# Weight places and loads of 8 KB a partition, and one float32 product in place of three fp32r ones

## Chip, cores and metric

The program runs on one core of one Trainium2 chip. The metric is the device time of one execution in microseconds (us). Engines: TensorE does the matrix products (PE, with PEld for its weight loads), VectorE (DVE), ScalarE (ACT) and GpSimd (POOL) work element by element, SyncE (SP) issues most of the DMA transfers. A "record" is one instruction in the trace.

## What is computed

One decoder layer on 512 tokens of width 1024, all of it float32: a projection whose columns feed four causal mixers (SSD, RWKV7, GLA, mLSTM), an output projection, LayerNorm, a router that sends each token to 4 of 32 experts, the experts, a gate, and LayerNorm again. Cut to what matters here:

```python
u = x @ w_in                                    # 1024 -> columns of the four mixers
u_ssd, u_rwkv, u_gla, u_mlstm = _split(u, (SSD_W, RWKV_W, GLA_W, MLSTM_W))
...
mix = jnp.concatenate([y_ssd, y_rwkv, y_gla, y_mlstm], -1) @ w_out      # 1024 x 1024
x = _layer_norm(DEEPNORM_ALPHA * x + mix, ln1_g, ln1_b)
# experts: top 4 of 32, weights per expert w_gu 1024 x 2048, w_down 1024 x 1024
hg, hl = jnp.split(xblk @ w_gu[e] + b_gu[e], 2, axis=-1)
hg, hl = jnp.minimum(hg, 7.0), jnp.clip(hl, -7.0, 7.0)
y = ((hl + 1.0) * (hg * jax.nn.sigmoid(hg * 1.702))) @ w_down[e] + b_down[e]
...
h = DEEPNORM_ALPHA * x + ffn
h = h + jax.nn.sigmoid(h @ ple_gate_w) * (p @ ple_proj)                 # the last gate
x = _layer_norm(h, ln2_g, ln2_b)
```

## The kernel before

**The front (0 to about 405 us).** `mixers()` computes the projections and the four mixers. A projection is done in blocks. `split()` (L149 to L159) loads 512 KB of weights through SP, ScalarE copies them rounded to the type fp32r (`wh`, L157), and VectorE takes what the rounding left (`wl`, L158). The tokens `x` are split in the same way into `x0h` to `x3h` and `x0l` to `x3l`. `proj()` makes one of 18 blocks (tile `pj`, 128 x 512) out of three products of parts, wh x, wl x and wh xl, each over 8 steps of k (128 rows of the 1024): 24 matmuls of one record each, at the helper's line L144. `projt()` makes 5 groups of 4 blocks with the tokens on the partitions (`pt`, 128 x 256, again 24 matmuls a block). The mixers' outputs are split too (`finish_tm`, and for RWKV7 where `yo` is made, L487 to L492), since the output projection (`mixed()` and `wout()`, tile `mix`) is 3 x 64 such matmuls. In the middle of the front runs RWKV7's recurrence: eight steps, each of them U = W Tt, then S and WO from VU, then W for the next step, with copies on VectorE between them. A scheduler lays out the order of the instructions on each engine in the front; it fills the gaps with blocks of projections.

**The experts (about 405 to 1497 us).** `moe()` takes the 32 experts in the order of a table. An expert's tokens come in groups of 32: 18 experts have three groups and 14 have two. For a group `up()` multiplies by the gate and up weights (tile `gu`, L1297), `swiglu()` follows on VectorE and ScalarE, and `down()` multiplies again (tile `dn`, L1308); each product of 32 tokens uses a quarter of the array, so four run side by side. An expert has 24 units of weights of 128 x 1024 (4 KB a partition, 512 KB). They stand in a ring of 32 places, made of four pools (14 `rb`, 8 `r2`, 2 `wr`, 8 `r3`), four more while the front ends. `used()` marks a place as free and `pump()` at once issues the next load into it through SP (L1229); 15 units are loaded ahead while the front still runs. These float32 products are not split. The layer's second input goes through the same ring (`embed()`, tile `emb`, L1356: float32 products of 128 x 512), and so do the 8 units of the last gate's weights.

**The tail (1497 to 1577 us).** `gateweights()` splits the last gate's weights, `transposed()` (L1552 to L1555) brings 128 rows of `h` onto the partitions and splits them as `hh` (ScalarE) and `hl` (VectorE), and `finish()` makes three matmuls a step (L1596, L1597, L1598), sigmoid, LayerNorm and the stores.

Of the kernel before, what the change touches and what calls it, by code (L numbers as in the profile page):

```python
# [14 lines left out]
ALU = mybir.AluOpType  # L15
# [21 lines left out]
OPT = {"conv": ("sx0",), "lnt": ("vv","va","aa","va"), "lov": ("zb",), "pl": (0,5,8,13,16,21), "pt": (), "em": 20, "wk": 6, "ml": 0, "hold": 0, "gm": (0,), "pe": 0, "order": "SABZDIgvLqmoM", "wm": (10,8,0), "bn": (), "ad": (), "rb": (2,0,3), "pf": {(0,1):15}, "ex": 4, "xq": 1, "aq": 1,  "ap": 2, "t1": (8,8), "pa": 1,  "op": ((2,1),(0,))}  # L37
# [89 lines left out]
def mixers(tc, nc, A, rbp, dram, mix, ctx, ident, ones, tri, x1d, accd, R, dbg):  # L127
# [110 lines left out]

    def projt(name):

        i = GI[name]
        w = [split(A["wT"][i, h], [128, 4, 256], "w") for h in range(2)]
        for c in range(NT):
            tk = slice(128 * c, 128 * c + 128)
            p = ps("p", "pt")
            n = 0
            for a, b in ((0, xh), (1, xh), (0, xl)):
                for k in range(KT):
                    mm(p[:, 0:256], b[k // 2][:, k % 2, tk], w[k // 4][a][:, k % 4], start=(n == 0), stop=(n == 3 * KT - 1))
                    n += 1  # L250
            yield p[:, 0:256]
# [3 lines left out]
    def finish_tm(name, k, i, y, tag, pt="m"):  # L255

        if k // 2 not in Y:
            Y[k // 2] = (tl(tag, W2, name + "h", F32R), tl(tag, W2, name + "l", F32R))
        yh, yl = Y[k // 2]
# [5 lines left out]
        s.activation(yh[:, :, tk], pp_, AF.Copy)  # L265
        R["done"] = v.tensor_sub(yl[:, :, tk], pp_, yh[:, :, tk].bitcast(F32)).ins
# [14 lines left out]
    def rwkv():  # L281
# [106 lines left out]
        AQ = tl("rb", [128, 32, 32], "AQ")  # L388
# [39 lines left out]
        for c in range(8):  # L428
# [54 lines left out]
            yo = tl("rd", [128, 2, 128], "yo")  # L483
# [3 lines left out]
            v.tensor_mul(yo, yo, gg[:, :, t2])  # L487
            if i == 0:
                Y[1] = [tl("rb", W2, "y_rwkv" + x, F32R) for x in "hl"]
            Yr = Y[1]  # L490
            s.activation(Yr[0][:, :, t2], yo, AF.Copy)
            v.tensor_sub(Yr[1][:, :, t2], yo, Yr[0][:, :, t2].bitcast(F32))  # L492
# [566 lines left out]
def moe(ctx, tc, nc, A, ident, rbp, R, x1d, accd, ovt, ove, out, dbg):  # L1059
# [62 lines left out]
    wg = []  # L1122

    def gateweights():

        for k in range(KT):
            w = ring[len(srcs) - KT + k]
            pool, tag, n = [(R["pools"]["r3"], "r3", RING3), (R["pools"]["wr"], "wr", SLOTS["wr"])][k] if k < 2 else (rbp, "rb", SLOTS["rb"])
            hi, lo = (pool.tile([128, D], F32R, name=x, tag=tag, bufs=n) for x in ("wh", "wl"))
            s.activation(hi, w, AF.Copy)  # L1130
            v.tensor_sub(lo, w, hi.bitcast(F32))
            wg.append((hi, lo))


# [569 lines left out]
```

## Times and profile before

| | us |
|---|---|
| three runs | 1573.88, 1576.99, 1579.82 (median 1576.99) |
| the profiled execution | 1578.24 |
| its span, first to last instruction | 1576.4 |
| PE busy in it | 1462.9 (93%) |
| DVE, ACT, POOL busy | 522.9, 301.7, 218.2 |
| mean granted TensorE clock | 0.961 of full |
| DMA, mean over the span | 296 GB/s, 148012 packets |

The profiled execution lies 1.25 us above the median. PE is the busiest engine over the whole, yet that is a mean over stages: the DMA engines are nearly idle in the front and in the tail, and full for the 1056 us of the experts. The stages must be read apart. PE's busy time counts a matmul to its modelled end, so records overlap: the pitch of records that follow one another (start to start) is what one costs.

### The profile page before, as it was taken

Reading aid. Unit: us, or ns where it says so; the run is one execution under the profiler, and the core shown is the slowest. Engines: PE = TensorE matmul, PEld = TensorE weight load, DVE = VectorE, ACT = ScalarE, POOL = GpSimd, SP = SyncE. Lnnn points to the kernel's source line nnn. Section 1 sums busy time; section 2 is a strip of 40 time slices with the busy share of each in tenths; the row PEclk is TensorE's granted clock in tenths of the full one; section 3 lists DMA queues with packets and bytes.
Section 4 is the critical chain, followed back from the end, with each engine's and each line's share of the span. In section 5 each row is a group of like instructions: output and inputs, shape, how many; then the busy total and the mean of one; then the engine's idle time right before and its main releaser. Section 6 shows DMA issues by size and latency. Waiting matters only on the chain. (4 is left out here: it accounts for less than half of the span.)

```text
span 1576.4 us, 36036 instructions
## 1 busy us (share of the span) xinstructions
PE 1462.9 (93%) x14672; PEld 776.0 (49%) x14672; DVE 522.9 (33%) x1597; ACT 301.7 (19%) x632; POOL 218.2 (14%) x222
## 2 busy tenths in 40 slices
PE   9989999997799999999999999999999998999985
PEld 5769879886244433443334333334434343334364
DVE  5688875668521112111121111111121111111155
ACT  4343523523011111110111110101111110111120
POOL 1011211003011211211111111111111211111100
PEclk9899999997899999999999999999999999999998
DMA  4222311654979999999999999999999999999931
GB/s 165 61 67 64 113 44 52 235 224 159 346 275 366 360 387 393 380 390 379 381 384 382 369 380 376 383 382 378 335 389 388 379 387 373 390 380 392 390 104 42
DMA packets 148012, 466.13 MB, mean 296 GB/s; under 512 B 27121, under 2 KB 36162, under 8 KB 147810
## 3 DMA queue, kind: packets, MB, share of 16 engines
q1 hardware_dynamic: 131666, 442.08, 74.2%
q0 software_dynamic: 14992, 18.90, 5.8%
q8 instruction: 117, 1.92, 0.5%
q10 hardware_dynamic: 1184, 2.80, 0.5%
q14 instruction: 53, 0.43, 0.1%
HBM read 452.08 MB, written 18.43 MB: 298 GB/s over the span
## 5 line engine op out<-in xcount | busy, mean ns | idle before, releaser
L1297 PE MATMUL gu<-w,x 128*32 128x512 f32 x5248 | 627.4, 596 | 22.7 <-DMA w<-in_we_dram 21.7
L1297 PEld LDWEIGHTS gu<-w,x 128*32 128x32 f32 x5248 | 189.1, 119 | 442.6 <-issue 292.8
L1316 DVE TENSOR_SCALAR a<-gu 128x256 f32<-128x256 f32 x82 | 34.8, 425 | 895.8 <-PE gu L1297 895.8
L1308 PE MATMUL dn<-w,h 128*32 128x256 f32 x5248 | 304.0, 387 | 0.6 <-issue 0.6
L1308 PEld LDWEIGHTS dn<-w,h 128*32 128x32 f32 x5248 | 160.4, 112 | 121.0 <-issue 8.7
L1327 POOL DMA_INDIRECT accd<-y,ixs x82 | 128.0, 1561 | 357.9 <-ACT y L1326 330.2
L1317 ACT ACTIVATE c<-a 128x256 f32<-128x256 f32 x82 | 34.2, 417 | 631.7 <-DVE a L1316 630.1
L1208 POOL DMA_INDIRECT xg<-x1d,ixt x32 | 32.8, 1025 | 585.2 <-PE tr L1279 524.1
L1326 ACT ACTIVATE y<-dn,gate 128x256 f32<-128x256 f32 x82 | 36.7, 473 | 273.2 <-PE dn L1308 273.2
L1279 PE MATMUL tr<-ident,xg 96*128 96x96 f32 (+1 forms) x256 | 31.6, 251 | 31.3 <-ACT h L1267 18.1
L1279 PEld LDWEIGHTS tr<-ident,xg 96*128 96x128 f32 (+1 forms) x256 | 22.6, 142 | 42.3 <-ACT h L1267 24.8
L158 DVE TENSOR_TENSOR wl<-w,wh 128x1024 fp32r<-128x1024 f32 x28 | 34.2, 1220 | 15.0 <-ACT wh L157 14.9
L1320 DVE TENSOR_TENSOR b<-b,c 128x256 f32<-128x256 f32 x82 | 34.9, 425 | 5.4
L1264 PE MATMUL tr<-ident,b 128*128 128x128 f32 x164 | 32.3, 298 | 4.7 <-DVE b L1320 1.6
L1319 DVE SCALAR_TENSOR_TENSOR b<-b,a 128x256 f32<-128x256 f32 x82 | 34.5, 421 | 1.8
L157 ACT ACTIVATE wh<-w 128x1024 fp32r<-128x1024 f32 x28 | 29.5, 1053 | 25.6 <-PE pj L144 17.4
L1280 ACT ACTIVATE x<-tr 128x384 f32<-128x384 f32 (+1 forms) x64 | 27.7, 443 | 34.2 <-PE tr L1279 33.2
L1318 DVE TENSOR_SCALAR b<-gu 128x256 f32<-128x256 f32 x82 | 34.0, 415 | 0.0
L1267 ACT ACTIVATE h<-tr 128x256 f32<-128x256 f32 x82 | 29.4, 381 | 15.1 <-PE tr L1264 12.2
L1089 DVE TENSOR_SCALAR pt<-iotas,rankm 128x384 bf16<-128x384 bf16 (+1 forms) x132 | 30.9, 295 | 0.0
L1289 PEld LDWEIGHTS <-sel 96*32 96x32 bf16 x656 | 17.8, 98 | 21.7 <-issue 9.9
L1596 PE MATMUL gu<-wh,hh 128*128 128x512 f32 (+1 forms) x72 | 27.6, 387 | 0.3 <-ACT hh L1554 0.3
(650 smaller groups left out, 1683.5 us busy)
## 6 DMA issues: line engine op xcount, KB each, us to landing
w<-in_we_dram SPq DMA_DIRECT2D x768, 512.0 KB
w<-in_wA_dram SPq DMA_DIRECT2D x18, 512.0 KB
w<-in_wT_dram SPq DMA_DIRECT2D x10, 512.0 KB
wo<-in_wO_dram SPq DMA_DIRECT2D x8, 512.0 KB
w<-in_pgw_dram SPq DMA_DIRECT2D x8, 512.0 KB
x<-in_xT_dram SPq DMA_DIRECT2D x4, 512.0 KB
xt<-in_xt_dram SPq DMA_DIRECT2D x4, 512.0 KB
x1d<-xt ACTq DMA_DIRECT2D x4, 512.0 KB
```

The lines of the kernel that those rows point to most:

```text
L158: v.tensor_sub(wl, w, wh.bitcast(F32))
L1208: return g.indirect_dma_start(out=xg[TURN.index(e) % XG][0:n], out_offset=None, in_=x1d, in_offset=bass.IndirectOffsetOnAxis(ap=ixt[0:n, e ...
L1279: ordered(pe.transpose(p[:, n * k:n * k + n], xg[j % XG][0:n, c:c + 128], ident[0:n, 0:n]))
L1297: ordered(pe.matmul(p[32 * c:32 * c + 32], xT[:, k, g_:32 * GROUPS_OF[TURN[e]]:GROUPS_OF[TURN[e]]], w, start=False, stop=(k == KT - 1), ti ...
L1308: m = ordered(pe.matmul(p[32 * c:32 * c + 32, 0:256], hT[:, k % 2, 32 * (k // 2):32 * (k // 2) + 32], w, start=False, stop=(k == KT - 1), ...
L1316: v.tensor_scalar(a, p[:, 0:256], 7.0, None, op0=ALU.min)
L1317: s.activation(c, a, AF.Sigmoid, scale=1.702)
L1318: v.tensor_scalar(b, p[:, 256:512], 7.0, -7.0, op0=ALU.min, op1=ALU.max)
L1319: v.scalar_tensor_tensor(b, b, 1.0, a, op0=ALU.add, op1=ALU.mult)
L1320: v.tensor_mul(b, b, c)
L1326: last = s.activation(y, p[:, 0:256], AF.Copy, scale=gate[:, r, s_:s_ + 1]).ins
L1327: x = g.indirect_dma_start(out=accq, out_offset=bass.IndirectOffsetOnAxis(ap=ixs[:, r, s_:s_ + 1], axis=0), in_=y, in_offset=None, compute ...
```

## The change

**Ring.** A place, and a load into it, becomes 128 x 2048 (8 KB a partition, 1 MB); the arrays in memory are laid out so that a partition's 8 KB are one piece. There are 15 such places, and one more that is two old `wr` places with two loads of 4 KB a partition. The ring has the same number of bytes. An expert has 12 units in place of 24. In the front, the tiles of the pool `rb` share a place two by two (by a new table, `MATES`).

**Products.** No weight, token or mixer output is split any more. The projections, the output projection and the last gate use the float32 tiles as they are, in 8 matmuls a block where 24 stood. The copies `wh` and subtractions `wl` are gone, with those of the mixers' outputs and of the tail. Projection weights go alternately to two `wr` and four `wh` places as loaded.

```diff
@@ -24,17 +24,19 @@
...
-SLOTS = {"rb": 14, "xh": 8, "wr": 2, "wh": 2, "wl": 2, "zb": 4, "zc": 7, "yy": 2, "rc": 4, "rd": 6, "mc": 5, "md": 4}
+SLOTS = {"rb": 7, "xh": 8, "wr": 2, "wh": 4, "zb": 4, "zc": 7, "yy": 2, "rc": 4, "rd": 6, "mc": 5, "md": 4}
...
-RING2 = 8
-RING3, XG, AB = 8, 2, 2
+RING2 = 4
+RING3, XG, AB = 4, 2, 2
...
@@ -149,17 +165,14 @@
...
-    def split(src, shape, name, hi="wh", lo="wl", raw="wr"):
-        w = tl(raw, shape, name)
+    turns = [0]
+    def wload(src, shape, name="w"):
+        turns[0] += 1
+        w = tl("wr" if turns[0] % 3 == 0 else "wh", shape, name)
         sy.dma_start(w, src)
-        wh, wl = tl(hi, shape, name + "h", F32R), tl(lo, shape, name + "l", F32R)
-        s.activation(wh, w, AF.Copy)
-        v.tensor_sub(wl, w, wh.bitcast(F32))
-        return wh, wl
-    def wsplit(i):
-        return split(A["wA"][i], [128, KT, 128], "w")
+        return w
...
@@ -225,29 +239,23 @@
     def proj(name):
         i = BI[name]
-        wh, wl = w0 if i == 0 else wsplit(i)
+        w = w0 if i == 0 else wload(A["wA"][i], [128, KT, 128])
         p = ps("p", "pj")
-        n = 0
-        for a, b in ((wh, xh), (wl, xh), (wh, xl)):
-            for k in range(KT):
-                if i == 0 and n in (2, 4, 6):
-                    warm(OPT["wm"][1])
-                mm(p, a[:, k], b[k // 2][:, k % 2], start=(n == 0), stop=(n == 3 * KT - 1))
-                n += 1
+        for k in range(KT):
+            if i == 0 and k in (2, 4, 6):
+                warm(OPT["wm"][1])
+            mm(p, w[:, k], xh[k // 2][:, k % 2], start=(k == 0), stop=(k == KT - 1))
         return p
     def projt(name):
         i = GI[name]
-        w = [split(A["wT"][i, h], [128, 4, 256], "w") for h in range(2)]
+        w = [wload(A["wT"][i, h], [128, 4, 256]) for h in range(2)]
         for c in range(NT):
             tk = slice(128 * c, 128 * c + 128)
             p = ps("p", "pt")
-            n = 0
-            for a, b in ((0, xh), (1, xh), (0, xl)):
-                for k in range(KT):
-                    mm(p[:, 0:256], b[k // 2][:, k % 2, tk], w[k // 4][a][:, k % 4], start=(n == 0), stop=(n == 3 * KT - 1))
-                    n += 1
+            for k in range(KT):
+                mm(p[:, 0:256], xh[k // 2][:, k % 2, tk], w[k // 4][:, k % 4], start=(k == 0), stop=(k == KT - 1))
             yield p[:, 0:256]
     Y = {}
...
@@ -255,15 +263,13 @@
     def finish_tm(name, k, i, y, tag, pt="m"):
         if k // 2 not in Y:
-            Y[k // 2] = (tl(tag, W2, name + "h", F32R), tl(tag, W2, name + "l", F32R))
-        yh, yl = Y[k // 2]
+            Y[k // 2] = tl(tag, W2, name + "T")
         tk = slice(128 * i, 128 * i + 128)
         p = ps(pt, "yT")
         for j in range(2):
             pe.transpose(p[:, 128 * j:128 * j + 128], y[:, 128 * j:128 * j + 128], ident)
         pp_ = p[:, 0:256].rearrange("p (j t) -> p j t", j=2)
-        s.activation(yh[:, :, tk], pp_, AF.Copy)
-        R["done"] = v.tensor_sub(yl[:, :, tk], pp_, yh[:, :, tk].bitcast(F32)).ins
+        s.activation(Y[k // 2][:, :, tk], pp_, AF.Copy)
...
@@ -860,8 +868,7 @@
         tk = slice(128 * i, 128 * i + 128)
         for kk in range(2):
-            for y, u in ((0, 0), (1, 0), (0, 1)):
-                mm(p, Y[kq][y][:, kk, tk], w[u][:, kk], start=(first and kk + y + u == 0), stop=(last and kk + u == 2))
+            mm(p, Y[kq][:, kk, tk], w[:, kk], start=(first and kk == 0), stop=(last and kk == 1))
...
@@ -871,31 +878,43 @@
...
-    seq = ["rb"] * 7 + ["r2"] * RING2 + ["rb"] * (SLOTS["rb"] - 9) + ["wr"] * 2 + ["r3"] * RING3 + ["rb"] * 2
-    room = {**SLOTS, "r2": RING2, "r3": RING3, "pp": NT}
+        return wload(A["wO"][h, kq], [128, 2, 512], "wo")
+    seq = ["rb"] * 3 + ["r2"] * RING2 + ["rb"] * (SLOTS["rb"] - 4) + ["wr"] + ["r3"] * RING3 + ["rb"]
...
         R["at"][tag] = R["at"].get(tag, 0) + 1
-        return R["pools"][tag].tile([128, D], F32, name="w", tag=tag, bufs=room[tag])
+        if tag == "wr":
+            return [wrp.tile([128, D], F32, name="w", tag=tag, bufs=SLOTS[tag]) for _ in range(2)]
+        return R["pools"][tag].tile([128, 2 * D], F32, name="w", tag=tag, bufs=room[tag])
+    def loaded(w, src):
+        if isinstance(w, list):
+            for h in range(2):
+                sy.dma_start(w[h], src[:, D * h:D * h + D])
+        else:
+            sy.dma_start(w[:, 0:src.shape[-1]], src)
...
@@ -1236,10 +1241,16 @@
     srcs = []
     for e in range(E):
         if e == OPT["em"]:
-            srcs += [A["pT"], A["pproj"][0], A["pproj"][1]]
-        srcs += [A["we"][e, u] if e < 2 else (e, u) for u in range(24)]
-    srcs += [A["pgw"][k] for k in range(KT)]
-    base = lambda e: 24 * e + (3 if e >= OPT["em"] else 0)
+            srcs += [A["pT"], A["pproj"]]
+        srcs += [A["we"][e, u] if e < 2 else (e, u) for u in range(12)]
+    srcs += [A["pgw"][k] for k in range(KT // 2)]
+    base = lambda e: 12 * e + (2 if e >= OPT["em"] else 0)
+    def part(i, at, n):
+        w = ring[i]
+        return w[at // D][:, at % D:at % D + n] if isinstance(w, list) else w[:, at:at + n]
...
@@ -1293,22 +1304,21 @@
     def up(p, e, xT, g_, ks, last):
         for k in ks:
             for c in range(4):
-                w = ring[base(e) + 2 * k + c // 2][:, 512 * (c % 2):512 * (c % 2) + 512]
+                w = part(base(e) + k, 512 * c, 512)
                 ordered(pe.matmul(p[32 * c:32 * c + 32], xT[:, k, g_:32 * GROUPS_OF[TURN[e]]:GROUPS_OF[TURN[e]]], w,
                                   start=False, stop=(k == KT - 1), tile_position=(0, 32 * c)))
             if last:
-                used(base(e) + 2 * k)
-                used(base(e) + 2 * k + 1)
+                used(base(e) + k)
     def down(p, e, hT, ks, last):
         m = None
         for k in ks:
             for c in range(4):
-                w = ring[base(e) + 16 + k][:, 256 * c:256 * c + 256]
+                w = part(base(e) + 8 + k // 2, D * (k % 2) + 256 * c, 256)
                 m = ordered(pe.matmul(p[32 * c:32 * c + 32, 0:256], hT[:, k % 2, 32 * (k // 2):32 * (k // 2) + 32], w,
                                       start=False, stop=(k == KT - 1), tile_position=(0, 32 * c)))
-            if last:
-                used(base(e) + 16 + k)
+            if last and k % 2:
+                used(base(e) + 8 + k // 2)
         return m
     def swiglu(p):
...
@@ -1545,19 +1562,19 @@
     def transposed(src):
-        hi, lo = (r3.tile([128, KT, 128], F32R, name="h" + x, tag="r3", bufs=RING3) for x in "hl")
+        t = r3.tile([128, KT, 128], F32, name="hT", tag="r3", bufs=RING3)
         for h in range(2):
             p = bank("tr", "tr")
             for k in range(4):
                 pe.transpose(p[:, 128 * k:128 * k + 128], src[:, 512 * h + 128 * k:512 * h + 128 * k + 128], ident)
             p = p.rearrange("p (k t) -> p k t", t=128)
-            s.activation(hi[:, 4 * h:4 * h + 4], p, AF.Copy, scale=ALPHA)
-            v.scalar_tensor_tensor(lo[:, 4 * h:4 * h + 4], p, ALPHA, hi[:, 4 * h:4 * h + 4].bitcast(F32), op0=ALU.mult,
-                                   op1=ALU.subtract)
-        return hi, lo
-    with tc.issue_after(last):
-        gateweights()
+            if h:
+                v.tensor_scalar(t[:, 4 * h:4 * h + 4], p, ALPHA, None, op0=ALU.mult)
+            else:
+                s.activation(t[:, 4 * h:4 * h + 4], p, AF.Copy, scale=ALPHA)
+        return t
...
@@ -1592,10 +1611,7 @@
                 p = bank("gu", "gu")[:, :w]
                 with tc.issue_after(q) if i and h else ExitStack():
                     for k in range(KT):
-                        (xh, xl), (wh, wl) = [t[:, k] for t in hT], [t[:, n] for t in wg[k]]
-                        pe.matmul(p, xh, wh, start=(k == 0), stop=False)
-                        pe.matmul(p, xl, wh, start=False, stop=False)
-                        q = pe.matmul(p, xh, wl, start=False, stop=(k == KT - 1)).ins
+                        q = pe.matmul(p, hT[:, k], wg[k][:, n], start=(k == 0), stop=(k == KT - 1)).ins
...
     r["bias"] = np.concatenate([bg, a["exp_b_down"][0]], 1)
+    def pairs(z):
+        z = z.reshape(*z.shape[:-3], z.shape[-3] // 2, 2, 128, D)
+        return np.swapaxes(z, -3, -2).reshape(*z.shape[:-3], 128, 2 * D)
     if experts:
         gu = a["exp_w_gu"][0].reshape(E, KT, 128, 2, 2, 2, 256).transpose(0, 1, 4, 2, 5, 3, 6).reshape(E, 16, 128, D)
-        r["we"] = np.concatenate([gu, a["exp_w_down"][0].reshape(E, KT, 128, D)], 1)
+        r["we"] = pairs(np.concatenate([gu, a["exp_w_down"][0].reshape(E, KT, 128, D)], 1))
     r["pT"] = a["p"][0, 0].T.reshape(2, 128, T).transpose(1, 0, 2).reshape(128, 2 * T)
-    r["pproj"] = a["ple_proj"][0].reshape(2, 128, D)
-    r["pgw"] = a["ple_gate_w"][0].reshape(KT, 128, D)
+    r["pproj"] = pairs(a["ple_proj"][0].reshape(2, 128, D))[0]
+    r["pgw"] = pairs(a["ple_gate_w"][0].reshape(KT, 128, D))
```

On PE, this is the end of the first projections, with the first step of RWKV7 (`G`) behind them. Before:

```order
L144 MATMUL pj<-x0h,wh 128x512 x2
L144 MATMUL pj<-x1h,wh 128x512 x2
L144 MATMUL pj<-x2h,wh 128x512 x2
L144 MATMUL pj<-x3h,wh 128x512 x2
L144 MATMUL pj<-x0h,wl 128x512 x2
L144 MATMUL pj<-x1h,wl 128x512 x2
...
L144 MATMUL pj<-x3l,wh 128x512 x2
L144 MATMUL G<-AR_433,KB_435 128x128 x2
```

After (`x_122` to `x_125` are the tokens, unsplit, and `w` is a block's weights as loaded):

```order
L160 MATMUL pj<-x_122,w 128x512 x2
L160 MATMUL pj<-x_123,w 128x512 x2
L160 MATMUL pj<-x_124,w 128x512 x2
L160 MATMUL pj<-x_125,w 128x512 x2
L160 MATMUL G<-AR_313,KB_314 128x128 x2
```

The same seven blocks stand ahead of `G`, with 8 matmuls each.

On PE again, a step of RWKV7's recurrence (from `U` to `S` and `WO`). Before:

```order
L144 MATMUL U<-W,Tt_674 64x64 x4
L144 MATMUL pt<-wh,x2l 128x256
L144 MATMUL pt<-wh,x3l 128x256 x2
L144 MATMUL pt<-wh,x0h 128x256 x2
...
L144 MATMUL pt<-wh,x1l 128x256 x2
L144 MATMUL pt<-wh,x2l 128x256
L144 MATMUL S<-VU,KT 64x64 x4
L144 MATMUL WO<-VU,G_453 64x64 x4
```

After, a late step:

```order
L160 MATMUL U<-W,Tt_507 64x64 x4
L160 MATMUL S<-VU,KT 64x64 x4
L160 MATMUL WO<-VU,G_329 64x64 x4
L160 MATMUL WO<-VU,G_329 128x64 x4
L160 MATMUL WO<-SS,AR_313 128x128 x2
L488 MATMUL oT<-ident,on 128x128 x2
```

In five of the eight steps the projections between `U` and `S` have gone; they stand behind the recurrence now.

## Rows read from the trace of the kernel before

**Rows 1.** Windows by stage: from:to, length, busy time (records) of each engine, then clock, DMA.
```profile
core 0: us, PE busy (x) PEld busy (x) DVE busy (x) ACT busy (x) POOL busy (x), PEclk, DMA share, GB/s
9.00:62.00 53.00, 49.62 (x194) 35.27 (x192) 32.26 (x41) 28.68 (x35) 1.62 (x3) 0.97 0.28 99
62.00:146.00 84.00, 76.39 (x418) 65.05 (x419) 71.47 (x166) 27.52 (x53) 8.55 (x13) 0.86 0.26 74
146.00:333.00 187.00, 183.33 (x1421) 159.65 (x1422) 128.05 (x363) 73.75 (x156) 27.63 (x50) 0.98 0.36 117
333.00:405.00 72.00, 51.14 (x293) 43.43 (x295) 60.41 (x213) 21.58 (x45) 16.84 (x20) 0.72 0.56 217
...
441.00:1497.00 1056.00, 1006.91 (x11747) 413.26 (x11740) 163.76 (x629) 128.72 (x313) 155.94 (x111) 0.99 1.02 377
1497.00:1577.00 80.00, 55.55 (x268) 43.86 (x266) 46.63 (x99) 14.93 (x23) 1.46 (x1) 0.87 0.22 74
```
**Rows 2.** SP's waits, 700 to 1490 us: waited for, total us, times, longest.
```profile
SPq L1229 <- DMA w<-in_we_dram: 461.9, 511, 5.8
SPq L1229 <- PE gu L1297: 17.4, 68, 0.6
```
**Rows 3.** The engines' waits, 420 to 1505 us.
```profile
PE gu L1297 <- DMA w<-in_we_dram: 21.7, 60, 1.1
```
**Rows 4.** PE's timeline at the first `G`: start, us, instruction, idle before it.
```profile
62.68 0.49 PE L144 MATMUL G<-AR,KB 64*128 64x128 f32 x4 [2.80 <-DVE KB L335]
```
**Rows 5.** PE's timeline in a `pj` block at full clock.
```profile
188.47 0.61 PE L144 MATMUL pj<-x0h,wh 128*128 128x512 f32 x2
188.92 0.62 PE L144 MATMUL pj<-x1h,wh 128*128 128x512 f32 x2
```
**Rows 6.** PE's timeline in a `pt` block.
```profile
264.38 0.40 PE L144 MATMUL pt<-wh,x2h 128*128 128x256 f32 x2
264.62 0.40 PE L144 MATMUL pt<-wh,x3h 128*128 128x256 f32 x2
```
**Rows 7.** The tile `emb`: records, duration in ns (least, median, most), first and last start.
```profile
L1356 PE MATMUL emb<-w x32: 592/592/697, 1082.7 to 1122.2; 128*128 128x512 f32 x32
```
**Rows 8.** PE's timeline: float32 products of `emb`.
```profile
1107.41 2.74 PE L1356 MATMUL emb<-w 128*128 128x512 f32 x6
...
1119.11 3.70 PE L1356 MATMUL emb<-w 128*128 128x512 f32 x8
```
**Rows 9.** PE's timeline: a float32 product of 128 x 256, and two steps' `U`.
```profile
207.07 1.13 PE L144 MATMUL ga<-qb,la 128*128 128x256 f32 x4
208.13 0.68 PE L144 MATMUL U<-W,Tt 64*64 64x64 f32 x8
...
216.30 0.67 PE L144 MATMUL U<-W,Tt 64*64 64x64 f32 x8
```
**Rows 10.** Windows with the instructions of tile `pj` alone: PE, PEld, DVE, ACT.
```profile
9.00:62.00 53.00, 42.44 (x168) 32.45 (x168) 3.66 (x5) 4.45 (x7) 0.97 0.28 99
62.00:146.00 84.00, 31.71 (x120) 23.68 (x120) 8.09 (x11) 5.52 (x9) 0.86 0.26 74
146.00:333.00 187.00, 36.23 (x144) 28.02 (x144) 12.20 (x17) 3.00 (x4) 0.98 0.36 117
```
**Rows 11.** The same of tile `pt`.
```profile
62.00:146.00 84.00, 23.46 (x156) 21.85 (x156) 2.49 (x6) 2.29 (x6) 0.86 0.26 74
146.00:333.00 187.00, 45.39 (x324) 40.46 (x324) 0.82 (x2) 5.30 (x14) 0.98 0.36 117
```
**Rows 12.** The same of tile `mix`: PE, PEld, DVE.
```profile
146.00:333.00 187.00, 34.42 (x139) 25.50 (x140) 3.76 (x6) 0.98 0.36 117
```
**Rows 13.** The splitting of weights on the page: busy us, mean ns of one, idle before.
```profile
L158 DVE TENSOR_TENSOR wl<-w,wh 128x1024 fp32r<-128x1024 f32 x28 | 34.2, 1220 | 15.0 <-ACT wh L157 14.9
```
**Rows 14.** DMA packets in the experts, 600 to 1400 us: packets, MB, share of 16 engines.
```profile
q1 hardware_dynamic: 79748, 290.38, 94.3%
```
**Rows 15.** DMA packets while rows of 2 KB are stored, 1564 to 1568 us.
```profile
q1 hardware_dynamic: 288, 0.52, 35.8%
```

More of the change, by code (lines that the diff above doesn't have):

```diff
@@ L36 @@
 GROUPS_OF = [NS if r < BIG else NS - 1 for r in range(32)]
-OPT = {"conv": ("sx0",), "lnt": ("vv","va","aa","va"), "lov": ("zb",), "pl": (0,5,8,13,16,21), "pt": (), "em": 20, "wk": 6, "ml": 0, "hold": 0, "gm": (0,), "pe": 0, "order": "SABZDIgvLqmoM", "wm": (10,8,0), "bn": (), "ad": (), "rb": (2,0,3), "pf": {(0,1):15}, "ex": 4, "xq": 1, "aq": 1,  "ap": 2, "t1": (8,8), "pa": 1,  "op": ((2,1),(0,))}
+MATES = [('sgw', 'aa'), ('gg', 'rr'), ('rk', 'ep'), ('em', 'kp'), ('AR0', 'AR1'), ('KB0', 'KB1'), ('G0', 'G1'), ('G2', 'G3'), ('rv', 'Lx'),
+         ('Tt0', 'Tt1'), ('mq', 'mk')]
+OPT = {"conv": ("sx0",), "lnt": ("vv","va","aa","va"), "lov": ("zb",), "pl": (0,5,8,13,16,21), "pt": (), "em": 20, "wk": 6, "ml": 0, "hold": 0, "gm": (0,), "pe": 0, "order": "SABZDIgvLqmoM", "wm": (10,8,0), "bn": (), "ad": (), "rb": (2,0,3), "pf": {(0,1):7}, "ex": 2, "xq": 1, "aq": 1,  "ap": 2, "t1": (8,8), "pa": 1,  "op": ((2,1),(0,))}
 EMPTY = 4096.0
@@ L135, in mixers @@
     pg = mix.enter_context(tc.tile_pool(name="pg", bufs=1, space=PSUM))
+    open_ = {}
     def tl(tag, shape, name, dtype=F32):
-        return {"rb": rbp, "zb": wz, "zc": wz, "rd": wz, "wr": wrp, "yy": wq, "rc": wq, "mc": wq}.get(tag, wk).tile(shape, dtype, name=name, tag=tag, bufs=SLOTS[tag])
+        if tag == "rb":
+            key = next((m for m in MATES if name in m), dtype)
+            t = open_.pop(key, None)
+            if t is None:
+                t = rbp.tile([128, 2 * D], dtype, name=name, tag=tag, bufs=SLOTS[tag])
+                open_[key] = t
+                t = t[:, 0:D]
+            else:
+                t = t[:, D:2 * D]
+            names = "abcd"[:len(shape) - 1]
+            return t.rearrange(f"p ({' '.join(names)}) -> p {' '.join(names)}", **dict(zip(names, shape[1:])))
+        return {"zb": wz, "zc": wz, "rd": wz, "wr": wrp, "yy": wq, "rc": wq, "mc": wq}.get(tag, wk).tile(shape, dtype, name=name, tag=tag, bufs=SLOTS[tag])
     def ps(tag, name):
@@ L172, in mixers @@
     warm(OPT["wm"][0])
-    w0 = wsplit(0)
-    x2 = [split(A["xT"][:, 2 * h:2 * h + 2], W2, f"x{h}", "xh", "xh", "zb") for h in range(4)]
-    xh, xl = [x[0] for x in x2], [x[1] for x in x2]
+    w0 = wload(A["wA"][0], [128, KT, 128])
+    xh = [tl("xh", W2, f"x{h}") for h in range(4)]
+    for h in range(4):
+        sy.dma_start(xh[h], A["xT"][:, 2 * h:2 * h + 2])
     pv = mp.tile([128, NPV], F32, name="pv")
@@ L486, in rwkv @@
                                        op0=ALU.mult, op1=ALU.add)
-            v.tensor_mul(yo, yo, gg[:, :, t2])
             if i == 0:
[L489 to L492, printed above, removed]
+                yo0 = yo
+                v.tensor_mul(yo, yo, gg[:, :, t2])
+                continue
+            if i == 1:
+                Y[1] = tl("rb", W2, "y_rwkvT")
+                v.tensor_copy(Y[1][:, :, 0:128], yo0)
+            v.tensor_mul(Y[1][:, :, t2], yo, gg[:, :, t2])
             if dbg is not None and "y_rwkv" in dbg:
@@ L873, in wout @@
     def wout(h, kq, *tags):
-        return split(A["wO"][h, kq], [128, 2, 512], "wo", *tags)
-    seq = ["rb"] * 7 + ["r2"] * RING2 + ["rb"] * (SLOTS["rb"] - 9) + ["wr"] * 2 + ["r3"] * RING3 + ["rb"] * 2
-    room = {**SLOTS, "r2": RING2, "r3": RING3, "pp": NT}
+        return wload(A["wO"][h, kq], [128, 2, 512], "wo")
+    seq = ["rb"] * 3 + ["r2"] * RING2 + ["rb"] * (SLOTS["rb"] - 4) + ["wr"] + ["r3"] * RING3 + ["rb"]
+    room = {**SLOTS, "r2": RING2, "r3": RING3, "pp": NT // 2, "wr": 1}
     def raw(look=False):
@@ L1121, in moe @@
     state = {"pin": False}
[L1122 to L1132, printed above, removed]
     def ordered(m):
@@ L1346, in embed @@
     def embed(i, tag):
-        at = base(OPT["em"]) - 3
-        pT, *pw = ring[at:at + 3]
-        ppt.append(tp.tile([128, D], F32, name=f"pp{i}", tag="pp", bufs=NT))
-        tk = slice(128 * i, 128 * i + 128)
+        at = base(OPT["em"]) - 2
+        if i % 2 == 0:
+            t = tp.tile([128, 2 * D], F32, name=f"pp{i}", tag="pp", bufs=NT // 2)
+            ppt.extend((t[:, 0:D], t[:, D:2 * D]))
         for h in range(2):
@@ L1355, in embed @@
             for k in range(2):
-                ordered(pe.matmul(p, pT[:, 512 * k:512 * k + 512][:, tk], pw[k][:, n], start=(k == 0), stop=(k == 1)))
+                ordered(pe.matmul(p, part(at, 512 * k + 128 * i, 128), part(at + 1, D * k + 512 * h, 512), start=(k == 0), stop=(k == 1)))
             s.activation(ppt[i][:, n], p, AF.Copy)
         if i == NT - 1:
-            for i in range(3):
+            for i in range(2):
                 used(at + i)
@@ L1427, in overflow @@
                 v.tensor_add(d[:, 3:4], d[:, 3:4], d[:, 4:5])
+                half = {}
                 def big(name):
-                    return ring2.tile([128, D], F32, name=name, tag="r2", bufs=RING2)
+                    if name in half:
+                        return half.pop(name)[:, D:2 * D]
+                    t = ring2.tile([128, 2 * D], F32, name=name, tag="r2", bufs=RING2)
+                    if name in ("x", "act"):
+                        half[{"x": "xT", "act": "hT"}[name]] = t
+                    return t[:, 0:D]
                 x = big("x")
@@ L1553, in transposed @@
             p = p.rearrange("p (k t) -> p k t", t=128)
-            s.activation(hi[:, 4 * h:4 * h + 4], p, AF.Copy, scale=ALPHA)
-            v.scalar_tensor_tensor(lo[:, 4 * h:4 * h + 4], p, ALPHA, hi[:, 4 * h:4 * h + 4].bitcast(F32), op0=ALU.mult,
-                                   op1=ALU.subtract)
-        return hi, lo
-    with tc.issue_after(last):
-        gateweights()
+            if h:
+                v.tensor_scalar(t[:, 4 * h:4 * h + 4], p, ALPHA, None, op0=ALU.mult)
+            else:
+                s.activation(t[:, 4 * h:4 * h + 4], p, AF.Copy, scale=ALPHA)
+        return t
+    wg = [part(len(srcs) - KT // 2 + k // 2, D * (k % 2), D) for k in range(KT)]
     p = bank("gu", "warm")
```

20 lines of the change are left out of this document (11 added, 9 removed).

## The prediction

> **What bounds the kernel now.** I read the windows first, since the page's means mix stages. In the front PE is busy for 49.62 of 53 us, then 76.39 of 84, then 183.33 of 187; only in 333 to 405 us is it far from full (51.14 of 72), with VectorE at 60.41 [rows 1]. In the experts, 441 to 1497 us, the DMA engines show a share of 1.02, and PE 1006.91 of 1056. The tail has a DMA share of 0.22. So the same change meets a front that TensorE mostly bounds, experts that transfers bound, and a tail that is a chain on PE. Which it is in the experts, the waits of SP's queue tell: from 700 us on it waits 461.9 us for loads of its own that have not landed, and 17.4 us for places that PE has not freed [rows 2]. The ring is full of work for the DMA engines and never short of places, so what counts there is how fast bytes arrive. PE itself waits 21.7 us in all for a load [rows 3]. The timeline gives PE's price a record, by pitch.
>
> **One product against three.** In a `pj` block two fp32r records begin every 0.45 us, 0.227 us each [rows 5]; three make 0.68 us. The trace holds float32 products of the same shape: `emb` has 16 products and 32 records, so two records each [rows 7]. Six in a row last 2.74 us; less the last one's 0.592 us, five pitches are 2.15 us, 0.43 each [rows 8]. A float32 product so costs 0.86 us, 0.18 more than the three it replaces. The eight records from a start, 3.70 us, give 0.444, which is 0.21 more: the upper end. At 256 columns two fp32r records take 0.24 us, so three take 0.36 [rows 6]. For float32 there is an upper bound in `ga`: four records up to the start of `U` in 1.06 us, 0.265 each, 0.53 a product [rows 9]; the lower is half of 512 columns' price, 0.43. So +0.07 to +0.17 a product; I take +0.10, since fp32r's price also falls by nearly half (0.227 to 0.12), but `ga` is the nearer row. Fewer instructions do not help: each new one is two passes that last longer than the three old ones together.
>
> **The front.** *9 to 62 us:* 168 `pj` records [rows 10] are 56 products, +10.0 us. Against it, PE is idle 3.4 us here, and the first `G` waits 2.80 us for VectorE [rows 4], which loses its splits of 1.22 us each [rows 13]. I count +3 (-3 to +10). *62 to 146 us:* 120 `pj` and 156 `pt` records [rows 10, 11] are 40 and 52 products: +7.1 and +5.2 us, on a PE that idles 7.6 us and waits for a VectorE busy for 71.47 us, which gets lighter by some eight splits, 9.8 us. +2 (-5 to +8). *146 to 333 us:* 48 products `pj`, 108 `pt` [rows 10, 11] and 46 `mix` [rows 12], +8.5, +10.8 and +8.2, which is +28 on an engine that is 98% busy. The new order also takes the projections out from between `U` and `S` in five of RWKV7's eight steps. Such a step is a chain of small products and copies, and lasts at least until the next `U`: 8.2 us where no projection stood in it [rows 9]. Were half of that empty five times, it would be 20 us of holes. The projections that leave them come later, into gaps of the mLSTM part, so I price the move at nothing and keep +12 for the case that those gaps are none. +28 (+8 to +40). *333 to 405 us:* the rest of `mix` costs 3 us, and the splits of the out projection's weights and of the mixers' outputs leave a busy VectorE: 0 (-4 to +5). The front is +33 us (3 + 2 + 28).
>
> What speaks against so much: busy counts overlaps. By pitch, the 146 to 333 us hold 144 x 0.227 + 324 x 0.12 + 139 x 0.227 = 103 us of these three kinds, where the rows add up to 116 [rows 10 to 12]. About 13 us of the "busy" is drawn-out ends, so that PE may have 3.7 + 13, some 17 us of gaps, that added work could fill without moving anything; with the waits for splits inside them, I keep 20.
>
> **The ring.** Bytes stay, packets of 4 KB become packets of 8 KB in 15 of 16 places. What a packet costs beside its bytes comes from two rows. In the experts a packet of 3641 bytes on the mean takes 0.943 x 800 x 16 / 79748 = 151 ns [rows 14]; during the stores one of 1806 bytes takes 0.358 x 4 x 16 / 288 = 80 ns [rows 15]. That leaves 39 ns for 1000 bytes, and 9 ns a packet. 32 experts x 24 loads x 128 partitions are 98304 packets; 46080 fewer, at 9 ns on 16 engines, are 26 us. PE can use as much as it waits for loads: 21.7 us [rows 3]. I take -21 (0 to -33). Below it, nothing; above it, SP also issues half as many loads, and PE's idle time of 49 us is the roof. Twice as large a piece lands later by one piece's time when PE starves, but the engines do not idle for that, so I give it nothing.
>
> A sentence of the Trainium skill speaks against this gain: "DMA: Bandwidth & Descriptors", section "Where 436 GB/s comes from", says that between HBM and SBUF the HBM side binds at some 358 GB/s a core. This trace moves 377 GB/s over the whole stage [rows 1], which is above it, so the limit as stated doesn't hold here; by the rule the ring would give 0 and the sum would be as in the first rival. The same page, section "Why small descriptors are slow (HBM only)", gives a packet about 3 cycles beside one for each 32 bytes; by that estimate two packets of 131 cycles become one of 259, 1.1%, some 12 us where the rows make 26.
>
> **The tail.** The gate's 64 products, 56 of 512 columns and 16 half products of 256, cost 56 x 0.18 + 16 x 0.10 = +11.7 us on the chain, which runs from the first transposed row to the last gate product; the subtraction `hl` on VectorE goes from ahead of the second product (-0.7, an estimate: a little over half of the 1.22 us of a split twice as wide [rows 13]). +11 (+7 to +13).
>
> **Sum.** 1578.24 + 33 - 21 + 11 = 1601 for an execution like the profiled one, and with the 1.25 us by which it lies above the median, 1600.
>
> **Rivals.** *The ring gives nothing,* as the rate is one of bytes: 1600 + 21 = 1621. For it, a DMA share of 1.02 over the whole stage says only that the engines are full; against it, the two packet prices. *PE's gaps take the front's added work.* Place: 9 to 333 us. If VectorE and the waits for splits set the pace there and PE's busy time only looks full, the stages come out at -3, -1 and 28 - 20 = +8 us; with the ring at its full 26, 1578 + 4 - 26 + 11 = 1567, 1566 at the median: faster. It decides where the front adds less than 7 us while the ring gives all. For it, the 13 us of drawn-out ends and VectorE's 71.47 of 84; against it, three stages in a row with PE busy for 91% or more. *Both in part:* front +10 and ring -20, 1578 + 10 - 20 + 11 = 1579, 1578: no change.
>
> **From these to the numbers.** The forecast has a chance of 0.57, with its own range of 1587 to 1613; the ring without gain 0.11; the filled gaps 0.16; both in part 0.16. What differs by less than 0.5% (8 us) can't be told from no change with this kernel. Slower is then 0.57 + 0.11 = 0.68, same 0.16, faster 0.16. The range, 1567 to 1619, leaves out the far half of the first two rivals.
>
> **What would show it.** In the profile after: float32 `pj` records at a pitch of 0.43 us, two a product; the first `G` some 4 us later; the experts' first product some 33 us later; q1's packets in the experts about half as many, with GB/s up by 2%; the stretch from the first to the last expert product some 21 us shorter; the gate 11 us longer. The forecast is wrong if the experts start within 10 us of before, or if their stage keeps its 1056 us.

## Result and the profile after

The changed kernel takes 1615.3 us (median of four runs) against 1577.1 us: a ratio of 1.024 [1.021, 1.027], some 38 us slower. Its profiled execution took 1617.92 us with a span of 1616.1. The forecast was 1600 us with a range of 1567 to 1619. The measured time lies inside that range, though 2 us above the forecast's own part of it (1587 to 1613). The sum is right in its direction and in two of its three terms; the third hides two errors of opposite sign, so that the total comes out as near as it does is partly luck.

Three points cut both executions into the same pieces. The views of the tiles `gu` and `dn` give them (records; durations in ns: least, median, most; first and last start in us). Before:

```profile
L1297 PE MATMUL gu<-w,x x5248: 590/592/1061, 404.6 to 1484.1; 128*32 128x512 f32 x195
L1308 PE MATMUL dn<-w,h x5248: 377/379/634, 436.4 to 1493.9; 128*32 128x256 f32 x195
```

After, with the last gate in its third row:

```profile
L1308 PE MATMUL gu<-w,x x5248: 590/592/1061, 455.1 to 1514.4; 128*32 128x512 f32 x195
L1318 PE MATMUL dn<-w,h x5248: 377/379/634, 486.9 to 1524.2; 128*32 128x256 f32 x195
L1614 PE MATMUL gu<-w,hT x144: 379/592/1062, 1538.9 to 1598.4; 128*128 128x512 f32 x112, 128*128 128x256 f32 x32
```

The first expert product comes at 455.1 us where it came at 404.6: the front lost 50.5. From there to the last start of `dn` it takes 1069.1 us where it took 1089.3: the experts gained 20.2. The gate lasts 59.4 us where it lasted 49.8: 9.6 lost. Together these make +39.9 us, where the two spans differ by 39.7.

The same pieces of all kernels run here, in us, each from its profiled execution. "First" is the first start of a tile; the experts' stage runs from the first start of `gu` to the last of `dn`. A piece is that of one execution. The profiled executions of x2 and x3 lie 5.3 and 4.2 us below their medians, those of the changed kernel and of x4 2.6 and 5.0 us above theirs. A difference of a few us between two fronts is therefore not firm.

| kernel | first `G` | first `Q` | first `gu` | stage | gate | time (median) |
|---|---|---|---|---|---|---|
| before | 62.7 | 146.0 | 404.6 | 1089.3 | 49.8 | 1577 |
| after | 68.1 | 149.0 | 455.1 | 1069.1 | 59.4 | 1615.3 |
| x1: `mq`, `mk` in own places | 67.3 | 145.4 | 426.5 | 1068.2 | 59.3 | 1589.2 |
| x2: float32 products alone | 67.1 | 135.6 | 423.0 | 1088.6 | 59.3 | 1611.3 |
| x3: ring and places alone (gate float32) | 60.5 | 157.2 | 425.4 | 1067.0 | 58.9 | 1589.1 |
| x4: two loads a place | 67.9 | 148.8 | 454.5 | 1088.8 | 60.2 | 1632.8 |
| x5: half of the ring | 61.0 | 144.5 | 402.2 | 1078.0 | 49.8 | 1566.8 |
| x6: ten of sixteen places | 62.5 | 151.4 | 394.0 | 1072.1 | 50.4 | 1550.8 |
| x7: `G2`, `G3` in own places | 68.4 | 152.7 | 429.3 | 1068.0 | 59.9 | 1590.2 |
| x8: x1, block `small` after `G` | 67.6 | 141.1 | 427.7 | 1067.9 | 60.1 | 1588.9 |

**The products cost what was forecast.** PE's timeline after (start, us, instruction), in a `pj` block, in `pt` and in the gate:

```profile
204.78 3.60 PE L160 MATMUL pj<-x,w 128*128 128x512 f32 x8
300.15 3.19 PE L160 MATMUL pt<-w,x 128*128 128x256 f32 x14
1544.80 2.31 PE L1614 MATMUL gu<-w,hT 128*128 128x512 f32 x5
```

Less one last record of 0.62, 0.38 and 0.59 us, the pitch is 0.43, 0.216 and 0.43 us. Against [rows 5, 6] that is +0.18 a product of 512 columns and +0.07 of 256, the lower end; `ga` of [rows 9] was not the better guide.

**The experts.** Rows of after to [rows 14], [rows 2] and [rows 3]: the queue's packets from 600 to 1400 us; SP's waits from 700 to 1510 us; the page's row of the products, with PE's idle time behind the last bar:

```profile
q1 hardware_dynamic: 43567, 297.83, 92.8%
```

```profile
SPq L908 <- DMA w<-in_we_dram: 552.3, 261, 12.3
```

```profile
L1308 PE MATMUL gu<-w,x 128*32 128x512 f32 x5248 | 587.3, 600 | 37.5 <-DMA w<-in_we_dram 37.1
```

Packets are down from 79748 to 43567 and MB up from 290.4 to 297.8. SP still waits for its own loads above all (its waits for PE, line by line, are 8.3 us at most), so the stage is still bound by arrival. PE waits 37.1 us for loads where it waited 21.7, in 39 pieces of at most 2.2 us where there were 60 of at most 1.1; a load is now 1 MB. So PE's wait for loads grew while the stage got shorter, and my use of those 21.7 us as the roof of the gain was a lucky bound, no cause.

**The front.** Windows of after (from:to, length, busy us and records of PE, PEld, DVE, ACT, POOL; then granted clock, DMA share, GB/s), for [rows 1]. The first is the whole front, the second and third cut it at the recurrence's first `Q` and last `U`:

```profile
9.00:455.10 446.10, 415.86 (x1949) 267.67 (x1951) 244.31 (x726) 112.56 (x245) 53.72 (x82) 0.89 0.33 111
149.00:285.40 136.40, 127.30 (x853) 91.52 (x852) 77.66 (x261) 34.55 (x84) 28.09 (x50) 0.87 0.21 59
285.40:455.10 169.70, 151.75 (x659) 101.82 (x661) 86.50 (x284) 39.00 (x93) 17.98 (x21) 0.86 0.46 170
149.00:220.00 71.00, 71.00 (x448) 49.84 (x448) 37.01 (x111) 21.96 (x54) 14.67 (x23) 1.00 0.29 79
220.00:279.00 59.00, 49.90 (x385) 38.88 (x384) 39.38 (x148) 11.81 (x30) 13.41 (x27) 0.71 0.11 37
455.00:1525.00 1070.00, 1002.41 (x12057) 409.17 (x12050) 177.66 (x705) 129.69 (x317) 156.12 (x111) 0.98 0.99 381
```

The row from 220 to 279 us stands out. It is RWKV7's recurrence, from the first step whose projections the new order took away. The granted clock averages 0.71 there, so PE ran for more than half of it at 1.2 GHz, after it had been left with small products and gaps. Behind the recurrence stands what should have filled it. One row leads to the reason. The mLSTM's `mq` is written by ScalarE from a projection; before, and after:

```profile
L501 ACT ACTIVATE mq<-pj,pvh x2: 769/774/778, 217.0 to 217.7; 128x512 f32<-128x512 f32 x2
```

```profile
L509 ACT ACTIVATE mq<-pj,pvh x4: 771/777/778, 266.9 to 291.0; 128x512 f32<-128x512 f32 x4
```

Its products on PE were done by 220.6 us (the last `pj` before the gap), and yet ScalarE took them up only at 266.9. It had other work in between, so its queue was open; what ended was the life of another tile. ScalarE's timeline (start, us, instruction, in brackets the idle time before it and what ended it), and the row of the transposes at L427, which read `KB`:

```profile
259.20 0.38 ACT L471 ACTIVATE on<-WO 64x256 f32<-64x256 f32 x1 [4.63 <-PE WO L160]
260.79 0.42 ACT L481 ACTIVATE osq<-on 128x256 f32<-128x256 f32 x1 [1.21 <-DVE on L480]
266.95 1.45 ACT L509 ACTIVATE mq<-pj,pvh 128x512 f32<-128x512 f32 x2 [5.74 <-PE kT L427]
```

```profile
L427 PE MATMUL kT<-ident,KB x16: 272/330/477, 68.5 to 266.5; 128*128 128x128 f32 x16
```

`mq` begins at 266.95 us, just as the last transpose of `KB` ends (266.49 us and 0.42 more). The last one of `rv`, at 266.70, still runs then, so the place that `mq` got is that of `KB`. By the list of tiles that share the seven 8 KB places, `AR`, `KB`, `G0` with `G1` (and then `y_rwkv`), `G2` with `G3`, `rv` and `Tt` leave one place at most until the last step has been turned, and `mq` was not given it; which tile held it, no row here shows. The two unread `mq` blocks fill both PSUM banks that the kernel gives the projections, and `mk`, `mv` and `mo` wait behind them: the next `pj` record starts at 274.14 us.

### The profile page after: what moved, and what is told of

Read it like the earlier page. It is cut to its first block, busy times and chain, and to the rows that moved or that the text cites. A ratio compares the mean times of both kernels' runs of the same rounds, so it can differ in the third digit from the quotient of the medians.

```text
span 1616.1 us, 33617 instructions
## 1 busy us (share of the span) xinstructions
PE 1493.5 (92%) x14232; PEld 714.5 (44%) x14232; DVE 462.9 (29%) x1530; ACT 251.0 (16%) x576; POOL 218.3 (14%) x222
## 5 line engine op out<-in xcount | busy, mean ns | idle before, releaser
L1308 PE MATMUL gu<-w,x 128*32 128x512 f32 x5248 | 587.3, 600 | 37.5 <-DMA w<-in_we_dram 37.1
L1308 PEld LDWEIGHTS gu<-w,x 128*32 128x32 f32 x5248 | 172.2, 119 | 434.2 <-issue 332.2
L1318 PE MATMUL dn<-w,h 128*32 128x256 f32 x5248 | 308.5, 391 | 0.5 <-DMA w<-in_we_dram 0.5
L160 PE MATMUL pj<-x,w 128*128 128x512 f32 x288 | 134.6, 621 | 2.2 <-ACT tap L513 1.9
L160 PEld LDWEIGHTS pj<-x,w 128*128 128x128 f32 x288 | 56.2, 200 | 70.7 <-issue 66.8
L160 PE MATMUL pt<-w,x 128*128 128x256 f32 x320 | 73.2, 381 | 0.1
L160 PEld LDWEIGHTS pt<-w,x 128*128 128x128 f32 x320 | 59.4, 190 | 9.1 <-issue 1.1
L1614 PE MATMUL gu<-w,hT 128*128 128x512 f32 (+1 forms) x144 | 57.4, 554 | 0.6 <-ACT hT L1574 0.6
L1614 PEld LDWEIGHTS gu<-w,hT 128*128 128x128 f32 x144 | 27.4, 194 | 26.3 <-issue 24.4
L1275 PE MATMUL tr<-ident,b 128*128 128x128 f32 x164 | 32.1, 296 | 4.7 <-DVE b L1330 1.6
```

The source lines that it names most:

```text
L160: pe.matmul(o, l, r, start=start, stop=stop, **kw)
L1308: ordered(pe.matmul(p[32 * c:32 * c + 32], xT[:, k, g_:32 * GROUPS_OF[TURN[e]]:GROUPS_OF[TURN[e]]], w, start=False, stop=(k == KT - 1), ti ...
L1318: m = ordered(pe.matmul(p[32 * c:32 * c + 32, 0:256], hT[:, k % 2, 32 * (k // 2):32 * (k // 2) + 32], w, start=False, stop=(k == KT - 1), ...
L1614: q = pe.matmul(p, hT[:, k], wg[k][:, n], start=(k == 0), stop=(k == KT - 1)).ins
```

## Experiments

Two theories of the front stood against each other: that the places cost it (through `mq`), or that the products' price did.

**x1.** `mq` and `mk` go to two places of 4 KB that the splits left empty.

```diff
-            Z[nm] = tl("rb", W2, nm)
+            Z[nm] = tl("yy" if nm == "mq" else "xh", W2, nm)
```

> The changed kernel, with the tiles mq and mk of the mLSTM taken out of the pool rb into two 4 KB places that stand empty since the splits have gone. Theory of the places: mq shares a pool of seven 8 KB places, all full, and waits for rv until 267 us; its results sit in the two PSUM banks of the projections, so nothing fills the recurrence. Then mq is read at about 220 us, the first expert product moves from 455 to about 437 us, and the time falls from 1615 to some 1598 us. Theory of the price: the front is longer because each float32 product costs more; then the first expert product stays within 3 us of 455 and the time at 1615.

Measured: 1589.2 us, 1.007 [1.005, 1.009] of before. The first expert product moved from 455.1 to 426.5. `mq` is read early (the expectation took `rv` for the tile that it waits for; the rows above say `KB`), and the recurrence keeps its projections and the full clock. The windows are cut as above, at the first `Q` and the last `U`:

```profile
L509 ACT ACTIVATE mq<-pj,pvh x2: 777/777/777, 211.0 to 218.8; 128x512 f32<-128x512 f32 x2
```

```profile
9.00:426.50 417.50, 392.56 (x1957) 254.05 (x1959) 242.88 (x728) 112.77 (x245) 54.21 (x82) 0.95 0.35 118
145.40:326.40 181.00, 178.38 (x1126) 126.85 (x1125) 91.33 (x284) 47.93 (x116) 28.07 (x50) 0.99 0.22 69
326.40:426.50 100.10, 82.95 (x390) 55.80 (x392) 71.52 (x262) 26.11 (x61) 18.49 (x21) 0.81 0.64 241
```

So the wait for a place costs 28.6 us of the front's 50.5 in the profiled executions, and some 25 by the medians (an estimate: the times differ by 26.1 us, the stages by 0.9). I had expected 18.

**x2.** The kernel before with the products of the change, on its old ring and places.

```diff
-        wh, wl = w0 if i == 0 else wsplit(i)
+        w = w0 if i == 0 else wload(A["wA"][i], [128, KT, 128])
...
-        for a, b in ((wh, xh), (wl, xh), (wh, xl)):
-            for k in range(KT):
+        for k in range(KT):
```

> The kernel before with only the products changed: one float32 product of 8 steps in projections, output projection and last gate; ring and front places of 4 KB stay. Theory of the places: the price alone, first expert product at about 435 us (before 405), experts' stage 1089 us as before, gate 10 us longer: 1577 + 30 + 10 = 1617 us. Theory of the price: all 50 us of the front come from the products, first expert product at 455, 1577 + 50 + 10 = 1637 us.

Measured: 1611.3 us, 1.022 [1.019, 1.024]. Front +18.4, stage as before, gate +9.5. My 30 for the products was too much.

**x3.** The changed kernel with the splits and three fp32r products back in the front; the gate stays one product.

> The changed kernel with the fp32r splits and three products back in the whole front; ring and places of 8 KB stay, and the last gate stays one float32 product. Theory of the places: mq waits here too, so the front loses 10 to 18 us against before (first expert product at 415 to 423 us) though its products are the cheap ones; experts 20 us shorter, gate 10 longer: 1577 + 14 - 20 + 10 = 1581 us. Theory of the price: the front is as before (405), 1577 - 20 + 10 = 1567 us.

Measured: 1589.1 us, 1.010 [1.005, 1.015]. The front loses 20.8 us though its products are the cheap ones, more than the 10 to 18 expected (and 1581 us in time); `mq` is read at 253 us. The large places alone make the front longer, with either product.

By the pieces, then, the products alone cost the front 18.4 us (x2) and the places alone 20.8 (x3), and both together 50.5, which is 11.3 more than their sum. That excess isn't firm, since both executions lie below their medians by some us. An estimate from the medians, less the changes of stage and gate, gives 25 us for the products, 25 for the places and 49 for both. So either costs about half, and whether they make each other dearer stays open.

**x4.** A place of 8 KB is filled by two loads.

```diff
-        if isinstance(w, list):
-            for h in range(2):
-                sy.dma_start(w[h], src[:, D * h:D * h + D])
-        else:
-            sy.dma_start(w[:, 0:src.shape[-1]], src)
+        for h in range(src.shape[-1] // D):
+            sy.dma_start(w[h] if isinstance(w, list) else w[:, D * h:D * h + D], src[:, D * h:D * h + D])
```

> The changed kernel, but each 8 KB place is filled by two loads of 4 KB a partition; places, order and products as in the changed kernel. If the experts' 20 us come from the packets' fixed cost, they go again: stage from the first to the last expert product 1089 us, time 1635. If they come from larger places or from fewer waits of SP between loads, the stage stays at 1069 us and the time at 1615.

Measured: 1632.8 us, 1.035 [1.032, 1.037]; the stage is 1088.8 us again. Its packets, 600 to 1400 us:

```profile
q1 hardware_dynamic: 79657, 290.06, 94.0%
```

So the whole gain in the experts hangs on loads of 8 KB a partition in place of two of 4 KB; places and order were those of the changed kernel. x4 doesn't part the size of a packet from the number of loads, which it doubles too. A load shows 144 packets, 128 of its rows and 16 more: the changed kernel makes 365 loads fewer than before, and its queue has 52560 = 365 x 144 packets fewer. What the small loads cost is time on the DMA engines and no waiting between loads, as the engines' share is higher with them (94.0% against 92.8) while they move fewer bytes.

**x5.** Front, tail and products as before; 8 KB places in the pools `r2` and `r3` alone, while a unit that falls on `rb` or `wr` takes two old places.

```diff
-        return R["pools"][tag].tile([128, D], F32, name="w", tag=tag, bufs=room[tag])
+        if tag in ("wr", "rb"):
+            return [R["pools"][tag].tile([128, D], F32, name="w", tag=tag, bufs=SLOTS[tag]) for _ in range(2)]
+        return R["pools"][tag].tile([128, 2 * D], F32, name="w", tag=tag, bufs=room[tag])
```

> The kernel before, front and tail with the fp32r splits and its own 4 KB places, so with its own order of work; in the ring only the pools r2 and r3 have places and loads of 8 KB, and two old rb places (or wr places) take a unit as two loads of 4 KB. Theory of packets and places: half of the packets become 8 KB, so the experts' stage gets about 10 us shorter (1079 us), the front stays at 405 us, the gate at 50 us: 1577 - 10 = 1567 us. Rival, that the 20 us need a whole ring of large loads: stage 1089, time 1577.

Measured: 1566.8 us, 0.993 [0.991, 0.995] of before, with the stage at 1078.0: half of the packets, a little over half of the gain, as expected.

**x6.** As x5, with `AR0` and `AR1`, and `KB0` and `KB1`, two to a place.

> As the half ring, but AR0 with AR1 and KB0 with KB1, which live equally long, stand two to a place of 8 KB, so ten of the ring's sixteen places take 8 KB in one load. Theory of packets: stage 13 us shorter (1076 us). The order in the front changes with the pools: the first step of the recurrence moves behind 31 more projection products than before, so the front may give back some of it: 1577 - 13 + 5 = 1569 us; if pairs that live equally long cost nothing, 1564 us.

Measured: 1550.8 us, 0.983 [0.981, 0.986] of before, the fastest of all. The stage is 1072.1 (expected 1076) and the front 394.0, 10.6 us shorter than before, where I had expected it longer. Its order differs from that of before, and the start of the recurrence is later (`Q` at 151.4); why it is the better one wasn't settled.

**x7.** The changed kernel with `G2` and `G3` out of the pool.

```diff
-        G = [tl("rb", [128, 2, 4, 2, 64], f"G{i}") for i in range(NT)]
+        G = [tl("rb" if i < 2 else "xh", [128, 2, 4, 2, 64], f"G{i}") for i in range(NT)]
```

> The changed kernel, with the tiles G2 and G3 taken out of the pool rb into two 4 KB places of the pool xh that stand empty since the tokens are no longer split. Theory of the places: in the changed kernel the last products of G come at 86 us (75 in the kernel with float32 products alone), since the pair G2, G3 waits for a place, and what hangs on G comes 11 us later; and one place less is wanted, so mq finds one early. Then the last G ends at about 76 us, Q starts at about 137 us instead of 149, mq is read before 225 us, the first expert product comes at 423 us as in the kernel with float32 products alone, and the time is 1577 + 18 - 20 + 10 = 1585 us. Rival, that G and Q are late for lack of PE time behind the dearer products: Q stays at 145 to 149 us, and the first expert product at 426 us or later, 1589 us or more.

Measured: 1590.2 us, 1.009 [1.005, 1.012]. Half of the expectation falls: the last `G` comes even later (about 91 us) and `Q` at 152.7, so no place holds `G` back; in PE's order other blocks stand ahead of it. The other half holds: with one place more in the pool `mq` is read at 231 us, not 267, and the front loses 25.8 us of its excess, by another way than in x1.

**x8.** x1, with the block `small` held until the last `G` is issued.

> The kernel with mq and mk in places of their own, and the eight products of the block small held until after the last product of G (in the changed kernel this block, 8.5 us on PE, stands ahead of the last G products, and the chain on VectorE that leads to Q starts behind them). Theory that the order on PE, and no place, makes G late: last G at about 77 us, Q at 137 us (145 without), first expert product at 418 us (426 without), 1581 us. Rival, that Q is bound by VectorE's own work ahead of it: Q stays within 2 us of 145, first expert product at 424 to 428, 1589 us.

Measured: 1588.9 us, 1.006 [1.004, 1.009]. The last `G` is done at 79 us and `Q` comes 4.3 us earlier than in x1; the first expert product 1.2 us later. Theory and rival are each half right: the order does make `G` and `Q` late, but the end is where the rival put it (424 to 428 us), not at 418. So with float32 products an earlier start of the recurrence doesn't bring the end of the front forward. In x1, x2, x7 and x8 `Q` lies anywhere from 135.6 to 152.7 us, and the front ends within 423 to 429.

## Why the prediction came out as it did

**The ring (-21, measured -20.2).** Right in its size, and its cause, the cost of packets of 4 KB, holds as far as x4 can show it: with the small loads back, on the same places, the whole gain is gone. Whether a load of 8 KB saves by its larger packets or by being one load in place of two stays open. In the stage itself the queue has 107262 - 57157 = 50105 packets fewer, and 20.2 us on 16 engines are 6.5 ns each, less than the 9 ns of [rows 14, 15]; x5 gives 11.3 us for 26601, 6.8 ns, but x6 gives 17.2 us for 33197, 8.3 ns, so one price a packet doesn't explain all three. That I took 21.7 and not the 26 of the packets rested on the step "PE can use as much as it waits for loads". This step failed, as PE's wait grew to 37.1; that it made the term better was luck. The first rival, a rate of bytes alone, is out. So is, for this kernel on one core, the Trainium skill's limit of some 358 GB/s ("DMA: Bandwidth & Descriptors", "Where 436 GB/s comes from"): the stage of after moves 381 GB/s on the mean. The estimate of 12 us from the Trainium skill's 3 cycles a packet ("DMA: Bandwidth & Descriptors", "Why small descriptors are slow (HBM only)") was too low against the 20.2 measured.

**The tail (+11, measured +9.6).** Right. At 256 columns the products were sized by +0.10 and measured +0.07, which is 0.5 us of the difference; the rest wasn't looked into.

**The front (+33, measured +50.5).** Two steps failed, against each other.

The first: "I price the move at nothing and keep +12". I saw in the order that five steps lose their fillers, and argued that the work is merely done later. That missed the cause of the move and its price. The fillers are away because two finished blocks can't be read until a place comes free. Left alone, the recurrence does get shorter: from the first `Q` to the last `U` it takes 136.4 us, where it takes 181.0 with its fillers in x1. But what should have filled it then stands behind it, and the stretch up to the first expert product takes 169.7 us in place of 100.1. PE's records in the two fronts are nearly the same (1949 and 1957). It is busy with them for 415.9 us at a granted clock of 0.89 on the mean, in x1 for 392.6 at 0.95, and the rest of the 28.6 us, 5.3, is idle time. So most of the price of the move shows as the same work at a lower clock: the recurrence left alone runs at 0.71 from 220 to 279 us, where x1 keeps 0.99, and the stretch behind it, where the clock is low in both (0.86, and 0.81 in x1), is 69.6 us longer. The price is 28.6 us by x1 and 32.1 between x2 and the changed kernel, some 25 by the medians. The sharing of places stood in the change's own text, with the rows of the order pointing at it; I never asked when each pair is given up and who is next for the place. Nor does any term of the sum hold the clock, though [rows 1] show it at 0.86 and 0.72 in two stages of the front.

The second: the products' +33 were 18 us by x2's pieces, 22 by x1's, some 25 by the medians. By stages of x2, whose places are those of before, `G` comes 4.4 us later (forecast +3), and the stretch from `Q` to the first expert product takes 28.8 us more (forecast +28). Between them the forecast was +2 and x2 shows -14.8: `G` to `Q` takes 68.5 us where it took 83.3. Its window (columns as above), and the same with the records of `pt` alone (PE, PEld, DVE, ACT):

```profile
67.00:136.00 69.00, 64.32 (x271) 39.49 (x271) 54.84 (x136) 18.50 (x37) 6.57 (x9) 1.00 0.26 70
67.00:136.00 69.00, 14.38 (x64) 12.00 (x64) 1.67 (x4) 1.55 (x4) 1.00 0.26 70
```

So the order of x2 isn't that of before either. It has 32 `pt` products ahead of `Q` where before had 52 [rows 11], and the 40 `pj` in both. At 0.43 us the other 20 make 8.6 us, which are missing between `G` and `Q` and stand behind `Q`: the term after `Q` looks right only with them in it, which is luck. Of the 6 us that are left between `G` and `Q`, two things can be the cause: VectorE, which was busy for 71.47 of 84 us [rows 1] and without its splits for 54.84 of 69, and PE's clock, 0.86 before and 1.00 in x2. No run parts them. I had written down VectorE's numbers and the sign, and then let PE's busy time decide. That PE's sum of work sets the end of the front at 423 to 429 us fits x1, x2, x7 and x8 and wasn't tested.

**The rivals.** "PE's gaps take the added work" may have held in one stage (62 to 146 us), which got shorter in x2 with dearer products, but some of them had moved behind it; its sum is wrong. None of the rivals held what made the difference, a place that comes free late.

## What to carry over

When tiles are put together in larger places, list for each place the last reader of either half and the next tile that wants it: a place is free when both halves are, and a tile that waits for one also keeps the PSUM bank of the result it should take up. A change that pays in one stage can be taken there alone: 8 KB places in the pools that the front doesn't use, and pairs of equal life in the others, gave 1.7% where the whole change lost 2.4%. (Of x6's 27 us, 17.2 are the experts' stage and 10.6 a front that got shorter for a reason not settled.) Three fp32r products of 512 columns cost 0.68 us and one float32 product 0.86, so PE pays for leaving out the splits; a gain can only come where VectorE or ScalarE leads, and no run here shows one for certain.

## What the runs showed of the hardware

- Loads of 8 KB a partition moved 2.6% more bytes in the same 800 us than twice as many of 4 KB (311.8 against 303.9 MB, after and x4, all queues), on a stage where the DMA share was about 1.
- A load of 128 rows shows 144 packets (365 loads fewer, 52560 packets fewer, before and after).
- PE's clock: in the recurrence with its projections the granted clock was 0.99 on the mean (x1, 145.4 to 326.4 us), in its steps without them 0.71 (after, 220 to 279 us).
- A float32 product of 256 columns has a pitch of 0.216 us a record in a row of `pt`, half of what it is at 512 columns (0.43).
